# An encoder layer with three mixers: stated engine orders in attention, earlier transfers, column scales as rows

## The chip, the cores and the metric

The kernel runs on one core of one Trainium2 chip. The metric is the device time in microseconds; the kernel before took 1168.31 us (median of three runs, 1164.31 to 1168.86). Engines are named PE (matrix products), ACT (activations and copies), DVE (element-wise and reductions), POOL (element-wise, slower) and SP, the SyncE queue from which nearly all transfers are issued.

## The reference

```python
h = rmsnorm(x, norm_g); u = h @ w_in          # 1024 tokens, 1024 -> 5312 columns
y_conv = conv_module(u_conv, ...)             # GLU, depthwise conv of 31, layer norm, silu
y_ret  = retention_branch(u_ret, ...)         # 4 heads of 128, chunks of 128, two directions
# latent attention: 8 heads, q and k of 128 plain + 64 rotary columns, v of 128
q  = rmsnorm(q_lat, qa_g) @ w_uq;  kv = rmsnorm(kv_lat, kva_g) @ w_ukv
s  = (q_nope . k_nope + rope(q_rope) . rope(k_rope)) * 192 ** -0.5
y_mla = softmax(s) @ v
y = concat([y_conv, y_ret, y_mla]) * silu(u_gate)
out = rmsnorm(x + y @ w_out, final_g)
```

All is float32. The kernel splits each operand of a product into a high part (rounded for PE's faster float32 form) and the rest, and makes three products of them (`mm3`): high by high, high by low, low by high.

## The kernel before

**Stage 1, input projection.** The input stays transposed on chip, eight tiles of 128 columns by 1024 tokens, split into `xH` and `xL` (`load_x`). The weights come in 21 units of 256 columns (`load_unit`, `run_unit`); a unit is 96 matmuls of 128 x 512. While the eight tiles arrive, unit 0 is multiplied tile by tile. `sq_x` squares each tile on ACT and adds the squares, on POOL but for the last tile. `row_rsqrt` turns the sum over the 128 partitions into 1 / root mean square per token: 8 matmuls (16 on the engine) whose weights are every eighth column of the sum and whose moving side is a single column of ones, a scale on DVE, a power on POOL, and a transfer to memory, from which the values are read back as a row over all partitions (`rbc`) and, for the first of the four uses, as columns (`rcol`). Convolution and retention run on DVE and ACT beside later units, handed out in pieces (`tick`).

**Stage 2, attention.** `lat` loads one half of a latent tile, scales it by the row of `row_rsqrt` (on POOL for the first half, `LATP`) and splits it. `g_k`, `g_q`, `g_v` and `g_r` project k, q, v and the rotary part of q for one head or pair of heads; `g_r` sends the rotary part through a transfer that swaps halves, `g_r2` multiplies with the cosine and sine tables on POOL and splits. `g_kr` does the shared rotary key. The weights come through `wload`: transfer, cast on ACT, split on DVE, in one call. A `Unit` is one head by 512 queries, 16 in all, each with eight slots. `qk(i)` makes five matmuls of scores; after every second slot DVE takes the row maximum and ACT the exponential with its row sum. `tr` transposes four 128 x 128 blocks on PE, copies them on ACT and splits them on DVE. `pvs` multiplies with v, `norm` brings the reciprocal of the row sums to a row, `fin` multiplies and stores. Projections of the next heads are spread over the slots by `slot_plan`; they share one bank (`up`) of the accumulation memory, the transposes have two (`pp`).

The row sums go to memory one float at a time and come back as a row:

```python
sp.dma_start(d.rearrange("(t p) -> p t", p=P), self.rs)
rb = mk(fin, [P, HS], tag="rb", bufs=1)
sp.dma_start(rb, d.rearrange("(o s) -> o s", o=1).to_broadcast([P, HS]))
tt(pool, self.g, self.g, rb, MUL)
```

**Stage 3, output projection.** `wo_load` and `y_load` fetch and split a slice of the output weights and of the mixed branches; `wo_mm` multiplies. The first five slices (`NWA`) are loaded in the slots of unit 15, through one raw buffer each for weights and branches. `finish` adds the input, normalises and stores.

**What sets the order.** The body is written in program order, and a planner with its own model of times orders the instructions of every engine (`schedule_with_timeline_sim`); program order is its priority. Each engine then runs its own list strictly in that order. Nothing in the kernel before fixes an order by hand.

Of the kernel before, what the change touches and what calls it, by code (L numbers as in the profile page):

```python
# [37 lines left out]
P_BUFS, PT_BUFS = 3, 2  # L38
# [3 lines left out]
PRO = ["up", "pp", "pp", "pv", "S", "S"]  # L42
LATP = [(i, 0) for i in range(5)]
# [5 lines left out]
SQD = (7,)  # L49
W2_BUFS = 11  # L50
NWARM = 12

# [4 lines left out]
def body(tc, xT, x, w_in, w_uqn, w_uqr, w_uk, w_uv, w_out, vecs, decay, final_g,  # L57
# [72 lines left out]
    def load_x(k, n):  # L130
        tf = mk(cv, [P, S + 2 * HALO], tag="hp", bufs=4)[:, :S]
# [134 lines left out]
    for k in range(KT):  # L266
# [15 lines left out]
        if k > 0:  # L282
            sq_x(k - 1)
    sq_x(KT - 1)
# [11 lines left out]
    def row_rsqrt(ss, scale, eps, o, d):  # L296
        col = mk(const, [P, KT], tag="rrc", bufs=2)
# [9 lines left out]
    row_rsqrt(ssx, 1.0 / D, EPS, rbc, r_dram)  # L307
    sp.dma_start(rcol, r_dram.rearrange("(t p) -> p t", p=P))
# [166 lines left out]
    ident = mk(const, [P, P], tag="ident")  # L475
    sp.dma_start(ident, idm[0])
# [159 lines left out]
    cosm = mk(wt, [P, S], tag="cosm")  # L636
    sinm = mk(wt, [P, S], tag="sinm")

    def wload(src, n, w, tag):
# [3 lines left out]
        sp.dma_start(r, src)  # L643
        act.copy(hi, r)
        split_l(dve, lo, r, hi)
        return hi, lo

    def lw_k(h):
        return wload(w_uk[h], KVT, P, "k")

    def lw_q(h):
        return wload(w_uqn[h], QT, P, "q")

    def lw_r(p):
        return wload(w_uqr[p], QT, P, "r")

    def lw_v(p):
        return wload(w_uv[p], KVT, 256, "v")

    W = {("k", 0): lw_k(0), ("v", 0): lw_v(0)}  # L660
    sp.dma_start(cosm, t_mla[0])
    sp.dma_start(sinm, t_mla[1])
    W["r", 0] = lw_r(0)
    W["q", 0] = lw_q(0)
# [10 lines left out]
    def lat_rows(h):  # L675
        rows[1, h] = row_bc(fin, "rb", lk_dram, h)
        rows[0, h] = row_bc(wt, "xh", lq_dram, h)

    def lat(i, h):
# [5 lines left out]
        tt(pool if (i, h) in LATP else dve, t, t, rows[int(i >= QT), h], MUL)  # L685
# [5 lines left out]
    lat(3, 0)  # L691
    lat(4, 0)
# [6 lines left out]
    for i in range(QT):  # L699
        lat(i, 0)  # L700
# [51 lines left out]
    def g_r(p, hf):  # L752
        o = up3(W["r", p], 0, QT, hf)
        xr = mk(wt, [P, HS], tag="xr")
        xs = mk(wt, [P, HS], tag="xs")
        act.copy(xr, o)
# [3 lines left out]
        rst[p, hf] = xr, xs  # L760

    def g_r2(p, hf):
        xr, xs = rst.pop((p, hf))
        tt(pool, xr, xr, cosm[:, half(hf)], MUL)
        tt(pool, xs, xs, sinm[:, half(hf)], MUL)
# [3 lines left out]
        a, b = sc("QA", 3, F32R), sc("QB", 3, F32R)  # L769
# [24 lines left out]
    class Unit:  # L794
# [6 lines left out]
        def qk(self, i):  # L801
# [13 lines left out]
            if j == 1:  # L815
                nm = mk(at, [P, 1], tag="nm", bufs=4)
                dve.tensor_reduce(nm, self.S, axis=AX.X, op=MAX, negate=True)  # L817
                p = mk(at, [P, S], tag="P", bufs=P_BUFS)
                act.activation(p, self.S, AF.Exp, bias=nm, accum_out=self.rs[:, t:t + 1])  # L819
                self.p.append(p)  # L820
# [12 lines left out]
        def norm(self):  # L833
            i = self.h * 2 + self.qh
# [3 lines left out]
            d = tc.dram_tile([HS], F32, name=f"rs_dram{i}")  # L838
            sp.dma_start(d.rearrange("(t p) -> p t", p=P), self.rs)
            rb = mk(fin, [P, HS], tag="rb", bufs=1)  # L840
            sp.dma_start(rb, d.rearrange("(o s) -> o s", o=1).to_broadcast([P, HS]))
            tt(pool, self.g, self.g, rb, MUL)

        def pvs(self, j):
            if j == 0:
                self.pv = ps("pv")
            p, c = self.h // 2, (self.h % 2) * P
            ph, pl = self.PT[j]
            for i in range(4):
                vh, vl = vv[p, 4 * j + i]  # L850
                mm3(self.pv, vh[:, c:c + P], vl[:, c:c + P], ph[:, i], pl[:, i], j + i == 0, j + i == 4)
# [5 lines left out]

    g_k(0, 0)
    lat_rows(1)
    lat(3, 1)  # L860
    lat(4, 1)
    g_v(0, 0)
    g_k(0, 1)
    g_r(0, 0)
    for i in range(QT):
        lat(i, 1)
    g_q(0, 0)
    g_kr()
    g_r2(0, 0)
    g_r(0, 1)  # L870
    g_r2(0, 1)

    lxx.close()
    sxx = ExitStack()
    def slot_plan(u):
        p, r = u // 4, u % 4
        a, b = 2 * p, 2 * p + 1
        last = p == MH // 2 - 1
        if r == 0:
            return {0: [lambda: W.update({("k", b): lw_k(b)}), lambda: g_q(a, 1)],  # L880
                    4: [lambda: g_v(p, 1)], 5: [lambda: g_v(p, 2)],
                    6: [lambda: W.update({("q", b): lw_q(b)})],
                    7: [lambda: g_v(p, 3)]}
        if r == 1:
            d = {0: [lambda: g_k(b, 0)], 1: [lambda: g_k(b, 1)], 4: [lambda: g_q(b, 0)]}
            if not last:
                d[2] = [lambda: W.update({("r", p + 1): lw_r(p + 1)})]
                d[6] = [lambda: g_r(p + 1, 0)]
                d[7] = [lambda: W.update({("v", p + 1): lw_v(p + 1)})]
            return d  # L890
        if r == 2:
            d = {0: [lambda: g_q(b, 1)]}
            if not last:
# [253 lines left out]
```

## Time and profile before

| | |
|---|---|
| median of three runs | 1168.31 us |
| the profiled execution | 1162.01 us |
| its span, first to last instruction | 1160.2 us |
| PE busy | 1115.4 us (96%) |
| DVE busy | 729.8 us (63%) |
| ACT busy | 408.2 us (35%) |
| POOL busy | 171.3 us (15%) |
| mean granted PE clock | 0.984 |
| moved by transfers | 101.33 MB |

A matmul's end is modelled in the trace, so busy PE overlaps from one matmul to the next; how far apart they start tells the rate. The clock of PE has two levels, 2.4 and 1.2 GHz, and the mean of a stretch tells how much of it ran at which. Releasers are inferred: "<-" names what ended an idle stretch last.

### The profile page before, as it was taken

Reading aid. Unit: us, or ns where it says so; the run is one execution under the profiler, and the core shown is the slowest. Engines: PE = TensorE matmul, PEld = TensorE weight load, DVE = VectorE, ACT = ScalarE, POOL = GpSimd, SP = SyncE. Lnnn points to the kernel's source line nnn. Section 1 sums busy time; section 2 is a strip of 40 time slices with the busy share of each in tenths; the row PEclk is TensorE's granted clock in tenths of the full one; section 3 lists DMA queues with packets and bytes.
Section 4 is the critical chain, followed back from the end, with each engine's and each line's share of the span. In section 5 each row is a group of like instructions: output and inputs, shape, how many; then the busy total and the mean of one; then the engine's idle time right before and its main releaser. Section 6 shows DMA issues by size and latency. Waiting matters only on the chain. (4 is left out here: it accounts for less than half of the span.)

```text
span 1160.2 us, 14263 instructions
## 1 busy us (share of the span) xinstructions
PE 1115.4 (96%) x5548; PEld 933.9 (80%) x5548; DVE 729.8 (63%) x998; ACT 408.2 (35%) x721; POOL 171.3 (15%) x147
## 2 busy tenths in 40 slices
PE   7999999999999999998899999899999979999997
PEld 6888888888898899886678787688778857888886
DVE  6699999997647785746765564555455553345033
ACT  6221222121334134223654453454454443333022
POOL 4300000212220442023201101010110000001000
PEclk9999999998999999999999999999999999999999
DMA  7212223221262122226212212121211242654213
GB/s 261 92 37 73 91 83 117 87 86 46 73 227 91 46 73 69 88 72 227 86 17 74 47 43 53 35 50 35 51 52 29 31 133 56 227 172 150 68 36 109
DMA packets 55491, 101.33 MB, mean 87 GB/s; under 512 B 15584, under 2 KB 19440, under 8 KB 55424
## 3 DMA queue, kind: packets, MB, share of 16 engines
q1 hardware_dynamic: 55376, 100.35, 27.6%
q8 instruction: 43, 0.70, 0.4%
q14 instruction: 24, 0.20, 0.1%
q0 software_dynamic: 48, 0.08, 0.1%
HBM read 74.14 MB, written 24.17 MB: 85 GB/s over the span
## 5 line engine op out<-in xcount | busy, mean ns | idle before, releaser
L176 PE MATMUL ps<-xL,wh 128*128 128x512 f32 (+1 forms) x612 | 240.2, 393 | 3.2 <-DVE xL L63 3.0
L177 PE MATMUL ps<-xH,wl 128*128 128x512 f32 (+1 forms) x612 | 239.6, 392 | 1.9 <-DVE wl L63 1.9
L175 PE MATMUL ps<-xH,wh 128*128 128x512 f32 (+1 forms) x612 | 238.9, 396 | 2.2 <-ACT xH L139 1.6
L63 DVE SCALAR_TENSOR_TENSOR acc<-hp,cwh,acc 128x1024 f32<-128x1024 f32 x120 | 153.3, 1317 | 0.3 <-DVE rrc L301 0.2
L176 PEld LDWEIGHTS ps<-xL,wh 128*128 128x128 f32 x612 | 116.6, 190 | 27.6 <-DVE xL L63 4.2
L177 PEld LDWEIGHTS ps<-xH,wl 128*128 128x128 f32 x612 | 116.1, 190 | 26.5 <-DVE wl L63 2.6
L175 PEld LDWEIGHTS ps<-xH,wh 128*128 128x128 f32 x612 | 116.0, 190 | 26.6 <-ACT xH L139 1.8
L63 DVE SCALAR_TENSOR_TENSOR PL<-ps,PH 128x512 fp32r<-128x512 f32 x128 | 85.7, 685 | 48.7 <-ACT PH L830 48.4
L175 PE MATMUL ps<-woH,yh 128*128 128x512 f32 (+1 forms) x264 | 99.2, 389 | 7.6 <-ACT yh L936 7.4
L176 PE MATMUL ps<-woL,yh 128*128 128x512 f32 (+1 forms) x264 | 101.4, 387 | 0.0
L177 PE MATMUL ps<-woH,yl 128*128 128x512 f32 (+1 forms) x264 | 100.3, 387 | 0.0
L830 ACT CAST PH<-ps 128x512 fp32r<-128x512 f32 x128 | 72.6, 590 | 69.9 <-PE ps L828 69.3
L817 DVE TENSOR_REDUCE nm<-ps 128x1 f32<-128x1024 f32 x64 | 78.1, 1221 | 29.8 <-PE ps L814 29.3
L819 ACT ACTIVATE P<-ps,nm 128x1024 f32<-128x1024 f32 x64 | 71.8, 1122 | 26.3 <-DVE nm L817 24.8
L828 PE MATMUL ps<-ident,P 128*128 128x128 f32 x512 | 73.2, 274 | 4.6 <-DVE PL L63 4.5
L828 PEld LDWEIGHTS ps<-ident,P 128*128 128x128 f32 x512 | 61.5, 141 | 18.0 <-DVE PL L63 6.9
L166 ACT CAST wh<-wraw 128x1024 fp32r<-128x1024 f32 x40 | 42.1, 1051 | 95.0 <-PE ps L176 92.1
L66 POOL TENSOR_TENSOR g<-g,rb 128x512 f32<-128x512 f32 x16 | 20.6, 1289 | 362.2 <-DMA rb<-rs_dram 201.4
L175 PEld LDWEIGHTS ps<-woH,yh 128*128 128x128 f32 x264 | 49.7, 188 | 19.2 <-ACT yh L936 8.4
L63 DVE SCALAR_TENSOR_TENSOR wl<-wraw,wh 128x1024 fp32r<-128x1024 f32 (+2 forms) x45 | 55.4, 1232 | 8.2 <-ACT wh L166 7.4
L177 PEld LDWEIGHTS ps<-woH,yl 128*128 128x128 f32 x264 | 49.7, 188 | 10.8 <-DVE yl L63 0.7
L176 PEld LDWEIGHTS ps<-woL,yh 128*128 128x128 f32 x264 | 49.7, 188 | 10.4
(280 smaller groups left out, 2056.9 us busy)
## 6 DMA issues: line engine op xcount, KB each, us to landing
wraw<-in_w_in_dram SPq DMA_DIRECT2D x40, 512.0 KB, 3.4
wor<-in_w_out_dram SPq DMA_DIRECT2D x16, 512.0 KB, 4.5
g_dram<-ga SPq DMA_DIRECT2D x29, 256.0 KB, 2.0
yr<-y_dram SPq DMA_DIRECT2D x18, 256.0 KB, 4.7
g<-g_dram SPq DMA_DIRECT2D x16, 256.0 KB, 3.4
rb<-rs_dram SPq DMA_DIRECT2D x16, 256.0 KB, 4.9
y_dram<-osb SPq DMA_DIRECT2D x16, 256.0 KB, 2.4
z<-in_x_dram SPq DMA_DIRECT2D x8, 512.0 KB, 3.7
```

The costliest lines, as they stand in the source:

```text
L63: eng.scalar_tensor_tensor(o, a, s, b, op0=op0, op1=op1)
L66: eng.tensor_tensor(o, a, b, op=op)
L166: act.copy(hi, t)
L175: pe.matmul(o, sh, mh, start=first, stop=False, skip_group_check=skip)
L176: pe.matmul(o, sh, ml, start=False, stop=False, skip_group_check=skip)
L177: pe.matmul(o, sl, mh, start=False, stop=last, skip_group_check=skip)
L817: dve.tensor_reduce(nm, self.S, axis=AX.X, op=MAX, negate=True)
L819: act.activation(p, self.S, AF.Exp, bias=nm, accum_out=self.rs[:, t:t + 1])
L828: pe.transpose(o[:, c * P:(c + 1) * P], self.p[t][:, (4 * j + c) * P:(4 * j + c + 1) * P], ident)
L830: act.copy(ph, o)
```

## The change

- From the first attention projection on, PE, ACT, DVE and SP run in program order (`manual_schedule`), up to the end of the attention; PE also to the end of the kernel. POOL, and everything before, is still ordered by the planner.
- The body of attention is put in a new order: projections and slots move, each slot makes its transposes one slot later, the exponential is emitted behind the transposes of its slot (`ex`), `pvs` goes in four parts over slots 2 to 5, `norm` splits into `rec` and `norm`.
- A weight load is split into `w_dma` and `w_cv`, which stand in different slots. The rotary tables are no longer kept whole; each `g_r` fetches the half that it needs.
- Row sums are transposed on PE, copied as four rows, and travel through POOL's queue. `row_rsqrt` reads contiguous weights, transposes its columns on PE and stores rows; the first use keeps its columns as `rcol`.
- Squares of the input come after all eight tiles, all added on DVE; tiles 4 to 7 have buffers of their own. The first halves of the latents are scaled on DVE.
- The first five slices of output weights are loaded and split in unit 14, slots 1 to 7; products with them fill slots of unit 15 and the end of attention.

```diff
-P_BUFS, PT_BUFS = 3, 2
+P_BUFS, PT_BUFS = 2, 3
+MAN = {mybir.EngineType.Activation, mybir.EngineType.DVE, mybir.EngineType.SP}
-        tf = mk(cv, [P, S + 2 * HALO], tag="hp", bufs=4)[:, :S]
+        tf = mk(cv, [P, S + 2 * HALO], tag="hp", bufs=4)[:, :S] if k < 4 else mk(cv, [P, S], tag="acc", bufs=4)
-            tt(dve if k in SQD else pool, ssx, ssx, tf, ADD)
+            tt(dve, ssx, ssx, tf, ADD)
-        if k > 0:
-            sq_x(k - 1)
-    sq_x(KT - 1)
+    for k in range(KT):
+        sq_x(k)
...
-            pe.matmul(c[:, n:n + 1], ss.rearrange("p (q n) -> p n q", n=KT)[:, n, :], ones[:, 0:1], start=True, stop=True)
+            pe.matmul(c[:, n:n + 1], ss[:, n * P:(n + 1) * P], ones[:, 0:1], start=True, stop=True)
         dve.tensor_scalar(col, c[:, :KT], scale, eps, op0=MUL, op1=ADD)
         pool.tensor_tensor(col, col, eps_c[:, :KT], op=ALU.pow)
-        sp.dma_start(d.rearrange("(p n) -> p n", n=KT), col)
+        pe.transpose(c[:KT, P:2 * P], col, ident)
+        row = mk(cv, [P, HS], tag="cb", bufs=2)[:KT, :P]
+        act.copy(row, c[:KT, P:2 * P])
+        sp.dma_start(d.rearrange("(n p) -> n p", p=P), row)
...
+    def w_dma(tag, i):
+        src, n, w = WSRC[tag]
         r = mk(wt, [P, HS], tag="wr", bufs=2)[:, :n * w].rearrange("p (n w) -> p n w", n=n)
+        sp.dma_start(r, src[i])
+        WR[tag, i] = r
+
+    def w_cv(tag, i):
+        src, n, w = WSRC[tag]
+        r = WR.pop((tag, i))
...
         act.copy(hi, r)
         split_l(dve, lo, r, hi)
+        W[tag, i] = hi, lo
...
-        tt(pool if (i, h) in LATP else dve, t, t, rows[int(i >= QT), h], MUL)
+        tt(dve, t, t, rows[int(i >= QT), h], MUL)
...
+        def rec(self):
             self.g = mk(fin, [P, HS], tag="g", bufs=2)
             sp.dma_start(self.g, g_dram[8 + self.h][:, half(self.qh)])
             dve.reciprocal(self.rs, self.rs)
+        def norm(self):
+            d = tc.dram_tile([HS], F32, name=f"rs_dram{self.h * 2 + self.qh}")
+            c = ps("pp")
+            pe.transpose(c[:4, :P], self.rs, ident)
+            row = mk(at, [4, P], tag="rr", bufs=1)
+            act.copy(row, c[:4, :P])
+            pool.dma_start(d.rearrange("(t p) -> t p", p=P), row)
             rb = mk(fin, [P, HS], tag="rb", bufs=1)
+            pool.dma_start(rb, d.rearrange("(o s) -> o s", o=1).to_broadcast([P, HS]))
             tt(pool, self.g, self.g, rb, MUL)
...
+    tail = ExitStack()
+    tail.enter_context(tc.manual_schedule(engines={mybir.EngineType.PE}))
+    inner = ExitStack()
+    if MAN:
+        inner.enter_context(tc.manual_schedule(engines=MAN))
+    g_kr()
+    w_dma("k", 1)
+    lat_rows(1)
     g_k(0, 0)
+    g_v(0, 0)
     lat(3, 1)
+    g_v(0, 1)
     lat(4, 1)
+    g_r(0, 0)
+    g_q(0, 0)
     g_k(0, 1)
+    w_cv("k", 1)
+    w_dma("q", 1)
+    g_r2(0, 0)
     for i in range(QT):
         lat(i, 1)
...
+        if r == 2:
+            return {0: [lambda: g_q(b, 1)], 2: C_("v", p + 1), 3: D_("q", a + 2), 4: C_("k", a + 2), 5: D_("k", b + 2),
+                    6: C_("q", a + 2) + [lambda: g_r2(p + 1, 0), lambda: g_k(a + 2, 0)], 7: [lambda: g_k(a + 2, 1)]}
+        return {0: [lambda: g_r(p + 1, 1)], 1: [lambda: g_q(a + 2, 0)], 2: C_("k", b + 2), 3: D_("q", b + 2),
+                6: [lambda: g_r2(p + 1, 1), lambda: g_v(p + 1, 0)]}
...
-            plan = {1 + k: [lambda k=k: wo_load(k), lambda k=k: y_load(0, k)] for k in range(NWA)}
+            plan = {1: [lambda: dma_k(0)]}
+            for k in range(NWA):
+                plan[3 + k] = [lambda k=k: cv_k(k)] + ([lambda k=k: dma_k(k + 1)] if k < NWA - 1 else [])
+        if u == NUN - 1:
+            ob = [None, None, None, [None, ps("up")]]
+            plan = {i: [lambda k=k: wo_mm(3, k, 1)] for k, i in enumerate((0, 1, 6, 7, 7))}
+            plan[7].append(lambda: wo_mm(3, 3, 1))
         for i in range(8):
             cur.qk(i)
+            if prev and i == 0:
+                prev.rec()
+            if prev and i == 1:
+                prev.norm()
+            q = (i - 3) % 8
+            if i >= 3:
+                cur.tr(q // 2, q % 2)
+            elif prev:
+                prev.tr(q // 2, q % 2)
+            if i % 2:
+                cur.ex(i // 2)
+            if prev and 2 <= i < 6:
+                prev.pvs(i - 2)
+            if prev and i == 5:
+                prev.fin()
             for f in plan.get(i, []):
                 f()
...
+    prev.rec()
+    prev.tr(2, 1)
+    prev.norm()
+    ob[0] = bank_pair(0)
+    for k in range(NWA):
+        for c in range(2):
+            wo_mm(0, k, c)
     prev.tr(3, 0)
     prev.tr(3, 1)
```

## Rows read from the trace of the kernel before

**Rows 1.** Busy time by stage; columns: stretch, its length, each engine's busy time (instructions), clock, transfers.

```profile
0.00:43.00 43.00, 35.24 (x160) 28.67 (x161) 33.64 (x48) 24.04 (x31) 17.57 (x21) 0.96 0.59 202
43.00:52.00 9.00, 9.00 (x34) 7.93 (x33) 1.39 (x2) 0.73 (x1) 1.68 (x1) 0.81 0.32 114
...
259.00:309.00 50.00, 50.00 (x205) 42.36 (x204) 33.85 (x45) 7.75 (x11) 12.90 (x8) 0.90 0.19 64
...
522.00:571.00 49.00, 40.85 (x169) 31.31 (x168) 32.85 (x44) 20.86 (x39) 14.49 (x10) 0.93 0.55 179
571.00:915.00 344.00, 330.55 (x1718) 275.28 (x1716) 191.99 (x277) 169.26 (x319) 43.97 (x34) 0.99 0.18 43
915.00:990.00 75.00, 66.52 (x312) 52.13 (x313) 36.32 (x48) 30.72 (x52) 2.64 (x3) 0.98 0.34 85
990.00:1131.00 141.00, 141.00 (x615) 115.06 (x614) 48.20 (x71) 37.96 (x65) 8.09 (x12) 1.00 0.39 133
```

**Rows 2.** What PE waited for, 0 to 43 us: total, times, longest.

```profile
PE ps L176 <- DVE xL L63: 3.0, 1, 3.0
PE ps L177 <- DVE wl L63: 1.9, 1, 1.9
```

**Rows 3.** Timeline of DVE and POOL in the start: start, length, engine, operation.

```profile
12.37 1.29 DVE L63 SCALAR_TENSOR_TENSOR xL<-hp,vec,xH 128x1024 fp32r<-128x1024 f32 x1 [0.17 <-ACT xH L139]
...
13.38 8.66 POOL L66 TENSOR_TENSOR cm<-cm,hp 128x1024 f32<-128x1024 f32 x3 [11.34 <-ACT hp L148]
...
19.76 3.36 DVE L63 SCALAR_TENSOR_TENSOR xL<-hp,vec,xH 128x1024 fp32r<-128x1024 f32 x1
```

**Rows 4.** Timeline of PE at 259 us.

```profile
259.76 3.74 PE L300 MATMUL ps<-ones,lss 128*128 128x1 f32 x16
...
267.17 0.77 PE L175 MATMUL ps<-xH,wh 128*128 128x512 f32 x1
267.74 0.63 PE L176 MATMUL ps<-xL,wh 128*128 128x512 f32 x1
268.17 0.63 PE L177 MATMUL ps<-xH,wl 128*128 128x512 f32 x1
```

**Rows 5.** Timeline of PE in attention, eight transposes and what follows.

```profile
923.74 1.04 PE L828 MATMUL ps<-ident,P 128*128 128x128 f32 x8
924.53 0.48 PE L810 MATMUL ps<-kH,qH 128*128 128x512 f32 x1
```

**Rows 6.** The line of the power: count, shortest, median and longest in ns.

```profile
L302 POOL TENSOR_TENSOR rrc<-rrc,epsc x4: 1637/1661/2636, 47.6 to 305.5; 128x8 f32<-128x8 f32 x4
```

**Rows 7.** Timeline, rotary part of the first query.

```profile
558.05 0.59 ACT L756 COPY xr<-ps 128x512 f32<-128x512 f32 x1
...
568.15 0.47 PE L813 MATMUL ps<-K,QA 128*128 128x512 f32 x1 [1.77 <-DVE QA L63]
```

**Rows 8.** Timeline, a late weight load and the row sums.

```profile
751.88 0.51 ACT L644 CAST whr<-wr 128x384 fp32r<-128x384 f32 x1 [8.84 <-DMA wr<-in_w_uqr_dram]
...
916.01 0.37 SPq L839 DMA_DIRECT2D rs_dram<-rs  x1
...
930.63 1.28 POOL L66 TENSOR_TENSOR g<-g,rb 128x512 f32<-128x512 f32 x1 [23.22 <-issue]
```

**Rows 9.** Page, costliest groups: busy us, mean ns of one, idle before.

```profile
L63 DVE SCALAR_TENSOR_TENSOR PL<-ps,PH 128x512 fp32r<-128x512 f32 x128 | 85.7, 685 | 48.7 <-ACT PH L830 48.4
...
L830 ACT CAST PH<-ps 128x512 fp32r<-128x512 f32 x128 | 72.6, 590 | 69.9 <-PE ps L828 69.3
L817 DVE TENSOR_REDUCE nm<-ps 128x1 f32<-128x1024 f32 x64 | 78.1, 1221 | 29.8 <-PE ps L814 29.3
L819 ACT ACTIVATE P<-ps,nm 128x1024 f32<-128x1024 f32 x64 | 71.8, 1122 | 26.3 <-DVE nm L817 24.8
```

**Rows 10.** Timeline of SP, output weights.

```profile
933.87 0.33 SPq L923 DMA_DIRECT2D wor<-in_w_out_dram  x1
...
939.91 0.33 SPq L923 DMA_DIRECT2D wor<-in_w_out_dram  x1
```

More of the change, by code (lines that the diff above doesn't have):

```diff
@@ L41 @@
 LTB = 3
-PRO = ["up", "pp", "pp", "pv", "S", "S"]
-LATP = [(i, 0) for i in range(5)]
+PRO = ["up", "pp", "pp", "pv", "S", "S", "up", "pp"]
 MAIN2 = ["pp", "pp"]
@@ L676, in lat_rows @@
         rows[1, h] = row_bc(fin, "rb", lk_dram, h)
-        rows[0, h] = row_bc(wt, "xh", lq_dram, h)
+        if h:
+            t = sc("QB", 3)
+            sp.dma_start(t, lq_dram[half(1)].rearrange("(o s) -> o s", o=1).to_broadcast([P, HS]))
+            rows[0, 1] = t
+        else:
+            rows[0, 0] = row_bc(wt, "xh", lq_dram, 0)
     def lat(i, h):
@@ L690, in body @@
     lat_rows(0)
-    lat(3, 0)
-    lat(4, 0)
+    for i in range(QT + KVT):
+        lat(i, 0)
     for h in range(2):
@@ L755, in g_r @@
         xs = mk(wt, [P, HS], tag="xs")
+        cs = [mk(wt, [P, HS], tag=g) for g in ("cosm", "sinm")]
+        for i in range(2):
+            sp.dma_start(cs[i], t_mla[i][:, half(hf)])
         act.copy(xr, o)
@@ L877, in slot_plan @@
         a, b = 2 * p, 2 * p + 1
-        last = p == MH // 2 - 1
+        more = p < MH // 2 - 1
+        D_ = lambda t, i: [lambda: w_dma(t, i)]
+        C_ = lambda t, i: [lambda: w_cv(t, i)]
         if r == 0:
[L880 to L883, printed above, removed]
-        if r == 1:
[L885 to L889, printed above, removed]
-            return d
+            if p == 0:
+                d = {0: [lambda: g_q(a, 1)], 1: [lambda: g_r(0, 1)], 2: [lambda: g_v(0, 2)], 3: [lambda: g_v(0, 3)],
+                     4: [lambda: g_k(b, 0)] + C_("q", b), 6: [lambda: g_r2(0, 1)]}
+            else:
+                d = {0: [lambda: g_q(a, 1)], 1: [lambda: g_k(b, 0)], 4: C_("q", b), 6: [lambda: g_v(p, 1)],
+                     7: [lambda: g_v(p, 2)]}
+            if more:
+                d[5] = D_("r", p + 1)
+            return d
@@ L891, in slot_plan @@
+        if r == 1:
+            d = {1: [lambda: g_q(b, 0)], 6: [lambda: g_k(b, 1)]}
+            if p:
+                d[0] = [lambda: g_v(p, 3)]
+            if more:
+                d.update({2: C_("r", p + 1), 3: D_("v", p + 1), 5: D_("k", a + 2), 7: [lambda: g_r(p + 1, 0)]})
+            return d
+        if not more:
+            return {0: [lambda: g_q(b, 1)]} if r == 2 else {}
         if r == 2:
[L892 to L897 removed]
@@ L909, in body @@
         plan = slot_plan(u)
-        if u == NUN - 1:
-            sxx.close()
+        if u == NUN - 2:
+            for f in plan.pop(0):
+                f()
             wtx.close()
@@ L931, in y_load, with y_cv @@
                     t = mk(rp[0], [P, HS], tag="yr", bufs=rp[2])
+                sp.dma_start(t, y_dram[k][:, half(hf)])
+                return t
+            def y_cv(hf, k, t):
                 pool_ = pa if k % 8 < NYA else rp[0]
@@ L993, in body @@
         y_load(0, k)
-    ob += [bank_pair(i) for i in range(2, 4)]
+    ob[2] = bank_pair(2)
     for k in range(NWA):
-        for st in range(2, 4):
-            for c in range(2):
-                wo_mm(st, k, c)
+        for c in range(2):
+            wo_mm(2, k, c)
+    ob[3][0] = ps("pv")
+    for k in range(NWA):
+        wo_mm(3, k, 0)
     for k in range(NWA, 8):
```

145 lines of the change are left out of this document (54 added, 91 removed).

## The prediction

> **What bounds the kernel now.** I read the busy time by stage first, then who waited for whom, then the timeline at the places where TensorE (PE) stands still. In the undisturbed stretch from 990 to 1131 us PE starts 615 matmuls in 141 us, 0.229 us each, and never stands [rows 1]; PE is the bound, and nearly all its work is the same after the change. So only what PE loses can move the time: its idle time, plus (1 - granted clock) times the length where the clock is down. By stage [rows 1]: 0 to 43 us, 7.8 idle and 1.7 clock; 43 to 52, 1.7 clock; 259 to 309, no idle but 5.0 clock; 522 to 571 (the entry into attention), 8.2 idle and 3.4 clock; 571 to 915 (units 0 to 13), 13.5 idle and 3.4 clock; 915 to 990 (the last two units), 8.5 idle and 1.5 clock. That is some 55 us, and no step can win more than its own part.
>
> The profiled execution took 1162.0 us (span 1160.2, about 2 around it); the median is 1168.3. I work out a difference against the profiled one and take it off the median.
>
> **The start.** PE's two long waits there are for a DVE split, 3.0 and 1.9 us [rows 2]. That split took 1.29 us alone and 3.36 us while POOL added squares, and POOL spent 8.66 us on three adds from 13.38 on [rows 3]. The change takes all adds from POOL and puts all squares behind the eight loads; loads 4 to 7 get tiles of their own, so they wait for no square. DVE gets six adds more (about 1.3 us each by the split's length, 8 us), off PE's path: what needs them is the row scale, and the second unit's matmuls (96 x 0.229 = 22 us) cover it; without that cover, 8 us would be late. Gone: 4.9 us of waits and most of the 1.7 of clock. I take **-5.5**, from -7 to +2 (the loads may be what is late next).
>
> **Column scales as rows.** Four times, 16 matmuls with one moving column run with weights picked eight floats apart. Two of these runs last 7.41 us (259.76 to 267.17) [rows 4], 0.232 us per matmul, so 64 take 14.8. Afterwards the weights are contiguous. No row has contiguous weights with one column; the nearest is the transpose, 128 contiguous weight columns, eight in 0.79 us [rows 5], 0.10 each. With 0.11 the 64 take 7.0: **-7.6**. Bounds: 0, if the step is not what costs, to -11 at half a transpose. Right behind these runs PE's matmuls are 0.43 us apart in place of 0.229 [rows 4], at the lower of PE's two clocks, 1.2 GHz: seven of them, 1.4 us, at each of three places (one in 43 to 52, two in 259 to 309 [rows 1]), 4.2 in all. The runs halve, so I take half of it off, **-2.5** (0 to -4.2). Added: a transpose in each of the four and in each of 16 units, 20 x 0.11 = **+2.2**. The four wait for POOL's power, 1.66 us [rows 6]; PE is held only if no other matmul stands between: **+1.5** (0 to 6.6).
>
> **Entry into attention.** The rotation tables no longer travel there whole, and the first five latent scalings leave POOL for DVE. But PE, ACT, DVE and SyncE now run in program order. The order is: K rope, one k, two v, one rope projection, one q, one k, then the first score tile, which needs the rotated query. From the evacuation of that projection to the matmul that uses it took 10.1 us (558.05 to 568.15) [rows 7]: a transfer, three POOL steps, a split. Queued on PE in between are 9 + 6 + 3 matmuls at 0.23, 4.1 us. On ACT the evacuation itself now stands behind the scaling of a latent tile that waits for DVE (about 2 us). So PE stands about 10.1 + 2 - 4.1 = 8 us. Then three latent tiles are scaled behind the rotated query on DVE (three times 0.7 + 0.7 + 0.7 in turn with ACT, 6.5 us) before the next q can end: 5 us more. With 2 for the first tiles that makes 15 us, against 11.6 idle and clock now, which count some 1.3 too little, since a modelled matmul end covers the first 0.17 of each gap: **+2**, from -5 (planned as well as now, without the 5 us) to +6 (the clock falls too).
>
> **Units 0 to 13.** The largest single loss begins on SyncE: ACT stood 8.84 us for a weight load (until 751.88), which was queued behind a row-sum transfer, and PE ran dry behind ACT. Such row-sum transfers take 14.6 us from issue to their use (916.01 to 930.63) [rows 8]. Afterwards weights are fetched two to five slots ahead and the sums go as four rows through POOL's queue. A slot is 5 score matmuls (1.15 us), 4 transposes (0.44), in four of eight slots 6 value matmuls (1.4), and at most one projection (0.23 x 9 or 6). I followed one unit of each kind through ACT (copy 0.59, exponential 1.12) and DVE (split 0.69, maximum 1.22) [rows 9]. Scores, maximum, exponential (3 us) have more than a slot before their transposes; no stall. The single bank of the projections stalls PE in two places: in the third unit of each head pair, slot 6, ACT and DVE first do a weight, the rope's four copies and splits, so the two k projections and the next one lose 2.0 us (three times); a v projection in neighbouring slots 7 and 0 loses 0.5 (three times). With 1.5 for unit 0 and 2 for late sums that is 11 against 16.9: **-6**, from -13 to +6 (2 us more in half the units).
>
> A rule of the Trainium skill speaks against POOL's queue (SBUF — State Buffer, section "SBUF: two separate sides"): while DVE runs an operation that takes the port pair it shares with POOL, the descriptors of a transfer issued from POOL can't be written. By it the two transfers of a unit would each wait for one DVE step at most, an estimate of 2 x 0.7 us, inside the slack; the trace shows the shared port only from the other side, DVE stretched from 1.29 to 3.36 us by POOL [rows 3].
>
> **The last two units.** Loads and conversion of five slices of the output weights move from unit 15 to unit 14, slots 3 to 7. They have one buffer: the next load is issued when the slice before is split. Load, cast, split turn in 6.04 us (933.87 to 939.91) [rows 10]. The slots last 3, 3, 3, 1.6, 1.6 us. In stated order ACT and DVE stand in slot 4 until the load lands, with the unit's copies and maxima behind them. The chain starts 8.4 us after slot 1, its fifth split ends at 8.4 + 4 x 6.04 + 3 = 35.6, and only then come the reciprocal and the transpose of the sums, for which PE waits; unhindered PE would be there at 20.3. So 15 us of stall, beside 2 of clock, against 10.0 now (with the same 1.3 hidden, 11 to 12). The partial products pulled into unit 15 fill PE later, not here. **+5**, from -6 (the loads are off the order's way) to +9.
>
> **Sum.** -5.5 - 7.6 - 2.5 + 2.2 + 1.5 + 2 - 6 + 5 = -10.9: 1162.0 becomes 1151, and the median **1157 us**. Projection and end are unchanged.
>
> **Rivals.**
> 1. The order runs clean: no wait of a whole slot stays. For it: PE has over half a slot of slack nearly everywhere. Against: the two chains of 10.1 and 6.04 us lie in the order. It gives -6 -10 +2 -8 -14 -9 = -45, 1123 us.
> 2. Slower: the row sums come too late. They start in slot 1, and the product with them is due at the end of slot 5, 12.4 to 14.5 us on, of which POOL needs 1.3. I reckon 7 to 8 us for the two transfers. If they take as long as now, 14.6 [rows 8], DVE stands 2 to 3 us at the unit's product with every split behind it, and PE loses about 2 us in each of 15 units: +30, 1187 us. It decides at 13 us. For it: each transfer waits for the one before, and POOL's other work stands in the same queue; against: 512 four-byte pieces become four rows.
> 3. The step of the weights costs nothing: the runs of 16 stay as long, and so does the clock. -10.9 + 10.1 = -1: 1167 us, no change that shows. For it: no row shows a short run; against: two to one in spacing to the transposes. The Trainium skill (SBUF — State Buffer, section "Door 1: The DMA port swizzle") speaks against it: only reads within one 16-byte line are at full rate, and eight floats apart each is on another line; the spacing of 0.232 against 0.10 us agrees.
>
> **How the numbers follow.** Forecast 0.45, rival 1 0.20, rival 2 0.20, rival 3 0.15. About 0.5% (6 us) is what can be told from no change here. The forecast's own range is 1146 to 1167 and 0.85 of it is faster, the rest the same; rival 1 is faster, rival 2 slower, rival 3 mostly the same. Faster 0.60, same 0.18, slower 0.22. The range that leaves out a tenth at each end reaches half-way into rivals 1 and 2: 1125 to 1180.
>
> **What would show it.** The runs of 16 at 1.8 us and not 3.7; no POOL add before 40 us, splits at 1.29; PE waiting for the rotated query some 8 us before the first unit; ACT waiting for output-weight loads in unit 14 and PE for the transposed sums about 9 us; the product in slot 5 not waiting for POOL. The forecast is wrong if PE's idle time from 522 to 990 us is under 10 or over 50 us.

## The result, and the profile after

The changed kernel took 1178.55 us (median of 5, 1174.51 to 1179.57) against 1168.31 for the kernel before beside it: ratio 1.009 [1.0065, 1.0114], slower by about 1%. Timed once more, beside later runs, it was 1.013 [1.011, 1.015]. The forecast was 1157 us, faster; the time lies just inside the outer range (1125 to 1180), the direction was wrong. The profiled execution took 1175.6 us.

Busy time of the kernel after by stage; columns as in [rows 1], stretches moved to where the same work now lies:

```profile
0.00:43.00 43.00, 41.65 (x200) 35.75 (x201) 29.61 (x56) 24.63 (x31) 3.47 (x16) 1.00 0.64 225
43.00:52.00 9.00, 9.00 (x42) 7.33 (x41) 2.35 (x4) 1.70 (x3) 2.31 (x1) 1.00 0.16 61
245.00:300.00 55.00, 55.00 (x258) 45.20 (x257) 45.79 (x56) 10.57 (x16) 18.49 (x10) 0.97 0.16 53
503.00:562.00 59.00, 46.49 (x188) 34.21 (x188) 34.89 (x53) 23.89 (x46) 8.87 (x9) 0.88 0.41 131
562.00:919.00 357.00, 346.34 (x1795) 282.84 (x1794) 204.05 (x286) 185.81 (x345) 59.44 (x63) 1.00 0.20 57
919.00:990.00 71.00, 57.89 (x259) 46.20 (x258) 27.44 (x36) 24.94 (x42) 5.98 (x7) 0.88 0.22 71
990.00:1014.00 24.00, 24.00 (x107) 19.83 (x106) 12.46 (x15) 10.55 (x14) 0.00 (x0) 1.00 0.88 317
1014.00:1047.00 33.00, 25.73 (x84) 16.92 (x82) 11.97 (x14) 9.08 (x13) 1.25 (x2) 0.79 0.37 123
1047.00:1140.00 93.00, 90.54 (x390) 72.67 (x389) 24.39 (x42) 18.84 (x38) 5.19 (x9) 1.00 0.25 82
```

The start is nearly full (1.35 us idle, clock 1.00). The surprise is 1014 to 1047: in [rows 1] PE never stands there, and now it is idle for 7.3 of 33 us at a mean clock of 0.79.

Busy time hides part of a gap and counts slow matmuls as busy. So from here I use PE's **loss**: from start to start of consecutive matmuls, less the usual distance of that form (0.229 us for 512 columns). The columns below are stretches of each kernel's own span; "work" is the sum of the usual distances, "first to last" the matmuls' whole. c1 and c2 are the two kernels run again, in two batches in which the kernel before had the same median (1159.6 and 1160.0 us). The runs come from several chips, so each row's ratio is to the kernel before timed beside it.

```
us of loss            0-80  240-320 520-600 600-920 920-1000 1000-end  work   first to last  ratio to before
before, first trace   12.7    3.5    13.5    21.9    13.7     1.1     1084.5   1152.5
after, first trace     4.0    2.8    24.4    16.4    19.4    18.8     1078.7   1165.8     1.009
c2 before again       16.1    3.6    13.7    16.3    12.8     0.9     1084.7   1149.8     1.000
c1 after again         3.5    1.2    24.4    16.3    19.0    19.2     1078.7   1163.6     1.013
e1 proj. planned       4.1    1.2    24.3    16.3    19.0     1.1     1078.7   1146.1     0.998
e7 slice by slice      4.2    2.9    24.6    16.3    19.2     5.5     1079.7   1154.1     1.002
e12 before + order    13.0    4.9    14.8    16.9    15.4    15.2     1084.5   1166.2     1.014
e5 slices spread       4.0    1.2    24.4    16.3     6.5    18.1     1078.7   1150.6     1.001
e3 only PE stated      4.2    4.5    21.3    19.8     2.7    19.4     1078.0   1151.7     1.001
e4 entry               6.2    1.2    23.8    16.4    19.5    18.6     1078.7   1165.8     1.012
e4b entry, space       6.4    1.3    21.8    16.4    18.9    18.6     1077.6   1162.8     1.010
e9 entry, full         4.5    1.2    13.5    20.5    13.7    20.3     1078.3   1153.4     1.002
e2 start + rows        5.8    2.8    15.6    17.3     9.7     1.0     1077.2   1130.6     0.982
e10 rows only         11.2    2.9    14.9    17.0    10.2     1.0     1078.2   1137.0     0.988
e11 start only         6.8    3.6    14.6    15.5    12.7     1.1     1084.3   1140.3     0.993
e6 three edits         6.0    4.3    22.4    16.4     6.5     1.2     1077.9   1136.4     0.985
e8 best                4.5    4.5    13.3    17.6     2.8     1.1     1077.7   1123.2     0.975
```

From c2 to c1: 0-80 us -12.6, 240-320 us -2.4, work -6.0, 520-600 us +10.7, 600-920 us nothing, 920-1000 us +6.2, projection +18.3, in all +14.

The stretches are fixed times, and the kernels reach a unit at different ones: unit 14 begins at 916.2 us in c2, at 907.1 in c1 and at 896.9 in e9. So a stretch can hold a neighbour's loss, and the same loss is counted once more between the first score matmuls of each kernel's own units: from 500 us to unit 1, from there to unit 14, and 85 us from unit 14 on.

```
us of loss             entry, unit 0   units 1-13   units 14, 15
before, first trace        13.2           22.0          13.7
c2 before again            13.4           16.4          12.9
c1 after again             21.2           18.7          19.4
e5 slices spread           21.4           18.6           6.9
e3 only PE stated          19.9           19.3           4.3
e9 entry, full             10.3           18.3          18.4
e2 start + rows            13.0           17.8          11.6
e8 best                    10.3           18.3           4.3
```

By this count the entry with unit 0 costs 7.8 us more from c2 to c1, units 1 to 13 cost 2.3 and the last two units 6.5.

**Projection.** PE's waits in the kernel after, 1014 to 1047 us (total, times, longest), then ScalarE's casts of the last slices of the output weights:

```profile
PE ps L174 <- ACT woH L952: 3.6, 5, 1.1
PE ps L175 <- DVE woL L62: 2.9, 5, 0.8
```

```profile
1018.03 1.05 ACT L952 CAST woH<-wor 128x1024 fp32r<-128x1024 f32 x1 [1.06 <-DMA wor<-in_w_out_dram]
1021.17 1.04 ACT L952 CAST woH<-wor 128x1024 fp32r<-128x1024 f32 x1 [2.10 <-DMA wor<-in_w_out_dram]
1024.17 1.04 ACT L952 CAST woH<-wor 128x1024 fp32r<-128x1024 f32 x1 [1.96 <-DMA wor<-in_w_out_dram]
...
1030.05 1.04 ACT L952 CAST woH<-wor 128x1024 fp32r<-128x1024 f32 x1 [2.08 <-DMA wor<-in_w_out_dram]
```

A slice is ready every 3 us. `finish(0)`, in program order, wants slices 8 to 15 for one half of one row block: three matmuls, 0.69 us, per slice. PE takes each slice as it comes and waits for the next, while all other banks' matmuls, whose slices are there, stand behind it. From 1024.3 us on, in the fifth such wait, the clock is at 1.2 GHz for 13.65 us. In the kernel before, the last cast began later, at 1035.67, and PE lost nothing: the planner had put other banks' matmuls between.

**Entry.** PE's waits from 515 to 570 us, then the chain that the first score tile waits for (QA holds the split of the rotated query, lH the high part of a latent):

```profile
PE ps L814 <- DVE QA L62: 7.7, 1, 7.7
PE ps L174 <- ACT lH L686: 2.7, 2, 1.8
PE ps L174 <- DVE xr L62: 1.6, 1, 1.6
```

```profile
539.60 0.57 ACT L757 COPY xr<-ps 128x512 f32<-128x512 f32 x1
...
548.15 0.62 ACT L769 CAST xh<-xr 128x512 fp32r<-128x512 f32 x1 [5.96 <-POOL xr L65]
...
549.63 0.77 PE L814 MATMUL ps<-K,QA 128*128 128x512 f32 x1 [7.67 <-DVE QA L62]
```

**Last two units.** The loads of the slices, and what PE waits for at their end:

```profile
928.03 0.33 SPq L948 DMA_DIRECT2D wor<-in_w_out_dram  x1
...
933.97 0.33 SPq L948 DMA_DIRECT2D wor<-in_w_out_dram  x1
...
940.15 0.33 SPq L948 DMA_DIRECT2D wor<-in_w_out_dram  x1
```

```profile
946.82 0.37 PE L845 MATMUL ps<-ident,rs 128*4 128x128 f32 x1 [7.36 <-DVE rs L840]
```

The cycle of [rows 10] stands again, 5.9 and 6.2 us, now with the reciprocal and PE's transpose in order behind its fifth turn.

### The profile page after: what moved, and what is told of

It reads as the page before. It is cut to its first block, busy times and chain, and to the rows that moved or that the text cites. A ratio compares the mean times of both kernels' runs of the same rounds, so it can differ in the third digit from the quotient of the medians.

```text
span 1173.7 us, 14356 instructions
## 1 busy us (share of the span) xinstructions
PE 1119.2 (95%) x5568; PEld 925.4 (79%) x5568; DVE 731.1 (62%) x1009; ACT 420.5 (36%) x741; POOL 168.0 (14%) x168
## 4 chain that ended last, share of the span: by engine, by line
PE 81%; DVE 6%; DMA 5%; ACT 5%; issue 1%; SPq 0%; POOL 0%; POOLq 0%; ACTq 0%; DVEq 0%
PE ps L174 22%; PE ps L175 21%; PE ps L176 21%; PE ps L832 4%; DMA wor<-in_w_out_dram 4%; PE ps L815 2%; PE ps L813 2%; PE ps L811 2%; PE ps L812 2%; PE ps L814 2%; DVE nm L818 1%; DVE woL L62 1%; ACT P L823 1%; ACT woH L952 1%; DVE vL L62 1%
## 5 line engine op out<-in xcount | busy, mean ns | idle before, releaser
L834 ACT CAST PH<-ps 128x512 fp32r<-128x512 f32 x128 | 75.0, 587 | 123.5 <-PE ps L832 123.4
L174 PE MATMUL ps<-woH,yh 128*128 128x512 f32 (+1 forms) x264 | 105.4, 399 | 6.7 <-ACT woH L952 3.6
L175 PE MATMUL ps<-woL,yh 128*128 128x512 f32 (+1 forms) x264 | 104.1, 394 | 2.9 <-DVE woL L62 2.9
L176 PE MATMUL ps<-woH,yl 128*128 128x512 f32 (+1 forms) x264 | 103.5, 392 | 0.1
L832 PE MATMUL ps<-ident,P 128*128 128x128 f32 x512 | 78.4, 277 | 5.6 <-ACT P L823 3.2
L174 PE MATMUL ps<-PH,vH 128*128 128x512 f32 x128 | 56.0, 437 | 0.0
```

The costliest lines, as they stand in the source:

```text
L174: pe.matmul(o, sh, mh, start=first, stop=False, skip_group_check=skip)
L175: pe.matmul(o, sh, ml, start=False, stop=False, skip_group_check=skip)
L176: pe.matmul(o, sl, mh, start=False, stop=last, skip_group_check=skip)
L832: pe.transpose(o[:, c * P:(c + 1) * P], self.p[t][:, (4 * j + c) * P:(4 * j + c + 1) * P], ident)
L834: act.copy(ph, o)
```

## Experiments

The question is where 25 us lie between the forecast of -10.9 and +14. Theory: three places where a stated order waits for a chain (projection, entry, last two units). Rivals differ by run.

**The projection.** e1 ends the stated order of PE with the attention:

```diff
     inner.close()
+    tail.close()
     atx.close()
...
-    tail.close()
     pax.close()
```

> The changed kernel with one edit: TensorE's stated order ends with the attention, so the output projection is planned again, as before the change. Theory A (the stated order makes TensorE wait for slices 11 to 15 one after the other while matmuls of other banks could run): the 18.8 us that TensorE loses in 1000-1160 us fall to about 1 to 5, 1178.5 - 14 to 18 = 1161 to 1165 us, and the low clock at 1024-1038 us is gone. Rival B (the slices arrive and are converted too late for any order, since the start of their loading moved): the loss stays, 1175 to 1180 us.

1158.33 us, 0.998 [0.996, 0.999]: by the changed kernel's two ratios (1.009 and 1.013) 13 to 18 us under it; 19.2 us of loss became 1.1. That planning does it and not the mere absence of an order is not yet shown. e7 keeps the order stated, and changes it:

```diff
-            for k in range(8, NG):
+            for k in range(13 if st < 4 else 8, NG):
...
+    for k in range(8, 13):
+        for st in range(4):
+            for c in range(2):
+                wo_mm(st, k, c)
     for st in range(4):
         finish(st)
```

> The changed kernel with TensorE's order still stated to the end, but in the first half of the projection slices 8 to 12 are multiplied into all eight banks, slice by slice, and only 13 to 15 bank by bank. Theory A (it is this order, in which one bank takes slices 8 to 15 one after the other while they arrive every 3 us, that costs the projection its time, not that it is stated): the loss in 1000-1160 us falls from 18.8 to 1-4 us and the low clock there goes, 13 to 17 us under the changed kernel, as where TensorE is planned. Rival B (a stated order as such loses there, because the planner adapts to arrivals in finer steps): 5 to 15 us of the loss stay.

1162.05 us, 1.002 [1.000, 1.003]. PE's row of 1000 to 1100 us in e7:

```profile
1000.00:1100.00 100.00, 98.33 (x427) 79.61 (x427) 34.71 (x51) 27.20 (x46) 4.49 (x8) 1.00 0.44 153
```

The waits for slices and the low clock go; 5.5 us of loss stay, which is the low end of rival B's range. Four waits of 0.94 to 1.04 us, each where a row block waits for VectorE to empty its bank, make up nearly all that e7 loses more than e1 (5.5 against 1.1). So it is this order that costs, and some 4 us are what the planner wins beyond it. e12 adds the order alone to the kernel before:

```diff
     prev.fin()
     atx.close()
+    tail = ExitStack()
+    tail.enter_context(tc.manual_schedule(engines={mybir.EngineType.PE}))
...
         finish(st)
+    tail.close()
```

> The kernel before with one thing added: TensorE runs the output projection in the order in which the program states it. Theory A (this order by itself costs what the changed kernel loses there): 13 to 18 us slower, ratio 1.011 to 1.016, the waits a slice apart near 1018 to 1035 us and a low clock stretch among them. Rival B (it costs only together with the changed kernel's later loads of the slices): 0 to 5 us.

1176.64 us, 1.0137 [1.0106, 1.0167]. PE's waits in e12, same stretch:

```profile
PE ps L175 <- ACT woH L924: 3.0, 3, 1.6
PE ps L176 <- DVE woL L63: 2.0, 4, 0.8
```

The cost needs nothing else of the change.

**The last two units.** e5 converts a slice every second slot of units 14 and 15:

```diff
-            for k in range(NWA):
-                plan[3 + k] = [lambda k=k: cv_k(k)] + ([lambda k=k: dma_k(k + 1)] if k < NWA - 1 else [])
+            cvp = {3 + 2 * k: [lambda k=k: cv_k(k)] + ([lambda k=k: dma_k(k + 1)] if k < NWA - 1 else [])
+                   for k in range(NWA)}
```

> The changed kernel with the five early slices of the output weights converted every second slot of units 14 and 15 instead of every slot of unit 14 (one raw buffer, whose reload takes about 6 us, a slot 5.6 us). Theory A (ScalarE and VectorE in a stated order wait for each slice's transfer, and the exponentials, copies and reciprocals behind them make TensorE wait 3.35, 2.18 and 7.53 us): the 19.4 us of loss in 920-1000 us fall to 8 to 12, and the clock with it, 1178.5 - 7 to 11 = 1167 to 1171 us. Rival B (the waits come from the row sums' and exponentials' own chains): 1176 to 1179 us; where slice 4 then comes too late for the projection, slower.

1163.54 us, 1.001 [1.000, 1.003]. PE's row of 920 to 1000 us in c1, then in e5:

```profile
920.00:1000.00 80.00, 67.51 (x299) 54.13 (x298) 32.30 (x42) 26.73 (x43) 4.84 (x6) 0.89 0.34 115
```

```profile
920.00:1000.00 80.00, 76.09 (x354) 61.99 (x353) 39.59 (x51) 33.08 (x53) 4.86 (x6) 0.98 0.46 162
```

Loss 6.5 against 19.0, less than the 8 to 12 expected, and slice 4 came in time. e3 asks which engine's order it was:

```diff
-MAN = {mybir.EngineType.Activation, mybir.EngineType.DVE, mybir.EngineType.SP}
+MAN = set()
```

> The changed kernel in which ScalarE, VectorE and SyncE are planned as before the change, and only TensorE keeps its stated order, to the end. Theory A (the projection's 18.8 us of loss come from TensorE's order alone; the waits of units 14 and 15 from ScalarE and VectorE standing in order behind the slices' transfers): 1000-1160 us lose 14 to 19 as in the changed kernel, 920-1000 us 8 to 12 instead of 19.4; 520-600 us stay at 20 to 26, because the first rotary query waits for a copy on ScalarE that no order of the others brings forward; the whole 5 to 12 us under the changed kernel. Rival B (the stated order of ScalarE and VectorE is what keeps the 14 middle units short, 16.4 us of loss against 21.9): those units lose 22 or more again and the whole is no better than the changed kernel.

1160.57 us, 1.001 [0.999, 1.002]. 920-1000 us lose 2.7, less than expected: what the changed kernel loses there is the order of the others, and the projection's loss (19.4) is PE's. The 19.8 against 16.3 from 600 to 920 us look like a gain of the others' stated order, but most of it lies at the stretch's ends: unit 1 loses 3 us before 600 us in c1, and unit 14 of e3 loses 1.7 before 920. Units 1 to 13 by themselves lose 19.3 in e3, 18.7 in c1 and 16.4 in c2. A gain of that order there is not shown.

**The entry.** e4 moves the first rotary product up, multiplies the three latents before it scales and splits them, and puts values 2 and 3 of unit 0 ahead of the second query:

```diff
     lat_rows(1)
+    g_r(0, 0)
     g_k(0, 0)
...
-    g_r(0, 0)
...
-    for i in range(QT):
-        lat(i, 1)
+    lt_ = [lat_a(i, 1) for i in range(QT)]
+    for i in range(QT):
+        lat_b(i, 1, lt_[i])
...
-                d = {0: [lambda: g_q(a, 1)], 1: [lambda: g_r(0, 1)], 2: [lambda: g_v(0, 2)], 3: [lambda: g_v(0, 3)],
+                d = {0: [lambda: g_v(0, 2)], 1: [lambda: g_v(0, 3)], 2: [lambda: g_q(a, 1)], 3: [lambda: g_r(0, 1)],
```

> The changed kernel with the entry into attention in another order: the first rotary product stands right behind the rotary key, so that its chain of copies, transfers and GpSimd products runs beside the first keys and values; the three scaled latents of the second half are multiplied first and split afterwards; in unit 0 the values go ahead of the second query. Theory A (what costs 24.4 us in 520-600 us is the chain of the first rotary query, 7.8 us of wait, then the latents one by one, 4.6 us, and the clock that falls in these waits): the loss falls to 8 to 14 us, 1178.5 - 10 to 16 = 1162 to 1168 us. Rival B (the wait only moves on to the latents or the values behind it): 1173 to 1179 us.

1175.33 us, 1.012 [1.010, 1.014]: nothing gained, the rival held. Timeline of e4:

```profile
536.00 0.59 ACT L763 COPY xr<-ps 128x512 f32<-128x512 f32 x1 [3.94 <-DMA g_dram<-xr]
```

```profile
536.61 2.48 SPq L766 DMA_DIRECT2D xs<-xr  x4
539.14 0.58 SPq L686 DMA_DIRECT2D osb<-l_dram  x1
```

The product was there at 530, but its copy waited for a store of unit 20 that still read the same memory; the rotary transfers waited for the copy, and the latents' loads stood behind them on SyncE. PE then waited 7.5 us for a latent instead. e4b takes both away (`lat_d` is a latent's load alone):

```diff
+        if (p, hf) == (0, 0):
+            t = mk(at, [P, S], tag="P", bufs=P_BUFS)
+            xr, xs = t[:, half(0)], t[:, half(1)]
...
+    lt_ = {i: lat_d(i, 1) for i in (3, 4, 0, 1, 2)}
     g_r(0, 0)
```

> The changed kernel with the entry's order changed as in the run before (first rotary product behind the rotary key, values ahead of the second query in unit 0), and two waits of that run taken away by other space and order: the copy of the product goes to a free buffer of the probabilities instead of one that a store of unit 20 still reads until 536 us, and the loads of all five latents of the second half are issued ahead of the rotary transfers. Theory A (the entry's cost is a chain: copy of the rotary product, its four transfers, three GpSimd products, split; it starts late because its buffer is held and it blocks SyncE's queue): the copy starts near 531-533 instead of 536-540 us, the wait for the first QA falls from 7.8 to 0-3 us, the loss in 520-600 us from 24.4 to 8-15, the whole 9 to 16 us under the changed kernel. Rival B (VectorE's work, some 19 us between 527 and 546, bounds the entry whatever the order): the loss stays at 18 to 24.

1172.31 us, 1.010 [1.009, 1.012]. Timeline of e4b:

```profile
532.17 0.59 ACT L767 COPY P<-ps 128x512 f32<-128x512 f32 x1
...
547.28 0.69 DVE L62 SCALAR_TENSOR_TENSOR QB<-P,xh 64x512 fp32r<-64x512 f32 x1
```

The copy starts 7.4 us sooner, the wait for QA falls only from 7.8 to 4.2, and the values wait 3.9 us for VectorE. The loss of 21.8 lies in rival B's range; expected was too much, for from the copy's start to the end of both splits the chain lasts 15.8 us. e9 gives PE work beside it (values, second query, second rotary product ahead of the scores) and the latents' products to GpSimd:

```diff
-        tt(dve, t, t, rows[int(i >= QT), h], MUL)
+        tt(pool if h else dve, t, t, rows[int(i >= QT), h], MUL)
...
     g_k(0, 1)
+    g_v(0, 2)
...
+    g_v(0, 3)
...
+    g_q(0, 1)
...
     g_r2(0, 0)
+    g_r(0, 1)
```

> The changed kernel with the entry of e4b taken further: GpSimd, idle there until 542 us, multiplies the five latents of the second half; values 2 and 3, the second query and the second rotary product all stand ahead of the first scores, so that TensorE has some 8.5 us more to do while the first rotary query's chain runs. Theory A (that chain, 14.4 us from the copy's end to QA and QB in e4b, is the entry's floor, and only work of TensorE beside it hides it): the wait for QA falls from 4.2 us (7.8 in the changed kernel) to 0-2, the values' 3.9 us to 0-1, the loss in 520-600 us from 21.8 (24.4) to 8-14, with the low clock there 3 to 7 us long instead of 13.65: 10 to 17 us under the changed kernel. Rival B (VectorE's splits, some 17 us from 527 on, stand in the way): loss 16 to 22, at most 8 us under the changed kernel.

1162.82 us, 1.002 [1.000, 1.004], and PE's row of 520 to 600 us in c1, then in e9:

```profile
520.00:600.00 80.00, 64.78 (x296) 48.36 (x295) 46.28 (x67) 36.90 (x68) 12.91 (x11) 0.91 0.26 84
```

```profile
520.00:600.00 80.00, 73.83 (x350) 57.75 (x349) 49.73 (x71) 43.56 (x81) 22.86 (x19) 0.96 0.31 97
```

The first scores wait 0.5 us for QA in place of 7.7; the loss is 13.5, as in the kernel before (13.7). Counted up to unit 1 it is 10.3, against 21.2 in c1 and 13.4 in c2. The 20.5 and 13.7 of the next two stretches are no change of those units: e9's unit 14 begins 10 us sooner, and part of its loss falls before 920 us.

**Start and row scales.** e10 has the row scales alone, e11 the start alone, e2 both, each on the kernel before (the diff's parts ahead of attention).

```diff
-            pe.matmul(c[:, n:n + 1], ss.rearrange("p (q n) -> p n q", n=KT)[:, n, :], ones[:, 0:1], start=True, stop=True)
+            pe.matmul(c[:, n:n + 1], ss[:, n * P:(n + 1) * P], ones[:, 0:1], start=True, stop=True)
...
-            tt(dve if k in SQD else pool, ssx, ssx, tf, ADD)
+            tt(dve, ssx, ssx, tf, ADD)
```

> The kernel before with the column scales as rows alone (contiguous weights for the matmuls of one column, a transpose, one transfer of rows); squares, attention and projection as before. The prediction's terms: -7.6 us for the 64 matmuls, up to -2.5 for the clock behind them, +2.2 for transposes, 0 to 6.6 for the power on GpSimd: -9 to 0 us, most likely -6.4, ratio 0.992 to 1.000. By the run that changed rows and start together (0.982, -21 us) what this run leaves is the start's share: forecast -5.5. Rival: the rows carry more than the matmul time, because the squares' sums reach them in time only then: -12 to -16 us, ratio 0.986 to 0.990.

> The kernel before with the start alone changed: squares added on VectorE, buffers of their own for the later slices of x. The prediction's term: -5.5 us (-7 to +2). By difference of the runs with rows and start (-21) and rows alone (-14): -7. Theory A (it lies in the first 52 us alone): loss in 0-80 us 12.7 to 5-7, the whole 5 to 8 us under the kernel before, ratio 0.993 to 0.9955. Rival (it also changes what is planned in attention): 10 or more, under 0.991.

> The kernel before with only the part of the change that lies ahead of attention: squares added on VectorE with buffers of their own, column scales computed as rows; attention and projection as before. Theory A (the parts add up, each pays where it lies): 8.8 us of loss at the start and 5.8 us of matmul time go, 1168.3 - 14 = 1153 to 1156 us. Rival B (the gain is given back behind it, since the transfers and TensorE's clock fall otherwise): 1163 to 1168 us.

e10 1145.71 us, 0.988 [0.986, 0.989]; e11 1151.34, 0.993 [0.990, 0.996]; e2 1140.39, 0.982 [0.979, 0.985]. They add up: 14 + 8 against 21 us, which is more than e2 was expected to give (12 to 15). e10's 14 us are the rival's number and more than its terms. By the traces (c2 to e10, -12.8): work -6.5, 240-320 us -0.7, and 40-80 us, where the low clock is gone, -2.5. The rest is spread (0-40 us -2.4, 920-1000 us -2.6, 520-600 us +1.2, 600-920 us +0.7), so the rival's cause isn't shown, and the stretch 0-40 us differs as much between the two traces of the same kernel before (11.2 and 13.4). c2 was run for that question:

> The kernel before once more, with a trace from the chip of the runs beside it: ratio 1.000. If part of what the row scales seemed to gain in attention was only that the first trace of before came from another chip, this trace loses 40 to 43 us in 520-1000 us, as e10; if the row scales' own effect reaches there, 47 to 50 as in the first trace.

Ratio 0.9998 [0.998, 1.002]; 42.8 us lost from 520 to 1000 us against 49.1 in the first trace. So what the row scales seemed to gain in attention (42.1 in e10) was the first trace's own.

> The changed kernel once more, as the common measure for the runs beside it: 0.7 to 1.1% over the kernel before, as in its first timing (1.009).

1174.72 us, 1.013 [1.011, 1.015], a little more than expected.

**A version that beats both.** e6 joins e1, e4b and e5; e8 joins e1 and e9 and ends the stated order of ScalarE, VectorE and SyncE at unit 14:

```diff
         if u == NUN - 2:
+            inner.close()
```

> The changed kernel with three edits together: TensorE planned in the projection, the slices spread over units 14 and 15, and the entry of e4b. Theory A (the three places are independent): losses of about 1 in the projection, 6.5 in 920-1000 us and 8 to 15 in 520-600 us, in all 33 to 42 us under the changed kernel, ratio to the kernel before 0.972 to 0.980: with or a little under the run that changes only the start (0.982). Rival B (spreading the slices leaves the projection less to do while slices 5 to 15 arrive, or the gains of one place reappear as waits in the next): 20 to 28 us under the changed kernel, 0.985 to 0.992.

> All that the runs so far point to: the start and the row scales of the change, the entry of e9, the stated order of all four engines kept for units 0 to 13 alone; from unit 14 on ScalarE, VectorE and SyncE are planned, in the projection TensorE too. Theory A (each place by itself): losses of 10 at the start, 8 to 14 in 520-600 us, 16 in units 0 to 13, 3 in 920-1000 us, 1 in the projection: 48 to 56 us under the changed kernel, ratio 0.963 to 0.971, under the run that changes only the start (0.982). Rival B (as e9's): 0.973 to 0.982.

e6 1143.89 us, 0.985 [0.983, 0.987]: faster than the kernel before, not than e2 (0.982); the entry still lost 22.4 where 8 to 15 were expected. e8 1130.74 us, 0.975 [0.973, 0.977]: faster than the kernel before and than e2. Its row of 920 to 1000 us:

```profile
920.00:1000.00 80.00, 78.19 (x363) 63.79 (x363) 35.85 (x45) 32.12 (x48) 4.83 (x6) 1.00 0.47 167
```

The places of e8 lost about what was expected of them (13.3, 17.6, 2.8, 1.1), the start less (4.5 against 10). The total in the expectation was not their sum: by the traces e8 lies 40 us under c1, by the medians 44, not 48 to 56, and the ratio lies where rival B had it. Against e2, which keeps attention as before, e8 loses 2.7 us less in the entry and 7.3 less in the last two units, and nothing less in units 1 to 13.

## Why the prediction was wrong

- **"Projection and end are unchanged"** is the step that failed: +18.3 us. I had read from [rows 1] that PE never stands in 990 to 1131 us and took that for a property of the work. It was one of the planner's order, and the change ended that too; the text even said that PE follows program order, and then followed it only to the end of attention. With this term at 18 the sum is +7, slower.
- **Entry: +2 forecast, +7.8 measured**, counted up to unit 1 (21.2 in c1, 13.4 in c2; the +10.7 of the fixed stretch holds 3 us of unit 1). The chain was right: 10.0 us from the copy (539.60) to the matmul (549.63), of which 8 us of wait were forecast (7.7), then 5 for the latents (4.1) and 2 for the first tiles (3.7). Left out was the clock while PE waits: 3.5 us of slow matmuls, which stood only in the upper bound. The rest, some 2 us, are small gaps that I did not assign.
- **Units 0 to 13: -6 forecast, no gain measured.** Units 1 to 13 lose 18.7 us in c1 and 16.4 in c2. What I worked out for the kernel after was right (11; idle and clock together are 10.7 in 562 to 919 us). The 16.9 of before was not: c2, the same kernel, has 12.9 in the same stretch, so by that count the gain is 2.2:

```profile
571.00:915.00 344.00, 334.56 (x1736) 279.14 (x1735) 193.71 (x279) 171.03 (x322) 43.95 (x34) 0.99 0.17 45
```

- **Last two units: +5 forecast, +6.5 measured**: 13.9 of wait and 5.1 of clock against "15 and 2".
- **Start: -5.5 forecast, -9.9 measured** from 0 to 40 us between c2 and c1; by e11 alone -8 in time. VectorE's splits lost GpSimd's interference and the loads were not late.
- **Row scales: -7.6, -2.5, +2.2, +1.5 forecast.** The runs of 16, kernel after:

```profile
249.10 1.84 PE L299 MATMUL ps<-ones,lss 128*128 128x1 f32 x16
250.81 1.93 PE L299 MATMUL ps<-ones,lsk 128*128 128x1 f32 x16
```

 1.8 us in place of 3.7 [rows 4]: rival 3 falls, and the work, transposes included, is 6.0 us less, against 5.4 forecast. The clock gave 5.1 from c2 to c1 (2.7 in 40-80 us, 2.4 in 240-320), twice the term, but part of that is luck of the trace: with the same row scales, 240-320 us lose 1.2 in c1 and 2.8 to 4.5 in the first trace, e2, e3, e6, e7, e8 and e10, against 3.6 in c2. In e3 the clock behind the runs is still at 1.2 GHz for 6.8 us. What stands against both traces of before are 1.5 to 2.7 us in 40-80 us, where the low clock is gone: about the term, and not twice it. The wait for the power is not seen. By the Trainium skill (SBUF — State Buffer, section "Door 1: The DMA port swizzle") reads within one 16-byte line go at full rate; the trace agrees for weights: contiguous columns cost 0.11 us a matmul, columns eight floats apart 0.23.
- **Rival 2** did not come. Row sums of one unit, kernel after:

```profile
634.79 0.55 POOL L848 DMA_DIRECT2D rs_dram<-rr  x1 [15.88 <-ACT rr L847]
637.16 0.58 POOL L850 DMA_DIRECT2D rb<-rs_dram  x1 [1.81 <-DMA rs_dram<-rr]
...
640.99 1.29 POOL L65 TENSOR_TENSOR g<-g,rb 128x512 f32<-128x512 f32 x1 [0.70 <-DMA rb<-rs_dram]
```

 6.2 us from issue to use where [rows 8] had 14.6 and the forecast 7 to 8 for the transfers. Rival 1 fell at both chains, 7.7 and 6.0 us.

In numbers, from c2 to c1: -10.9 plus 18.3 (projection), 5.8 (entry), 8.3 (units) and 1.5 (last two), less 4.4 (start), 0.6 (work), 2.6 (clock) and 1.5 (power) is +14. That the time still fell inside the outer range is luck: the range reached into rivals 1 and 2, and the mechanism of neither came.

Still open: what part of a stretch's low clock is cause and what effect of the waits. In the entry, the last two units and the projection it is lower where PE waits most, and no run took the one away without the other.

## What to carry to other kernels

Where a written order takes the place of a planned one, walk it to its last instruction, and at each stretch whose inputs arrive one by one, ask which ready work stands behind the first that isn't: a stretch without idle time in the old trace says nothing of the new order there. State an order by hand only where a run shows that it wins, and give the rest back. In units 1 to 13 no run shows it (18.7 us of loss in c1, 19.3 in e3, 16.4 in c2). In the last two units PE's stated order with the other engines planned loses 4.3 us (e3 and e8) against 12.9 in c2; which part of that is the order and which the earlier loads, no run separates. Count a stage between its own instructions and not between fixed times when kernels reach it at different ones. And a small gain read off one trace needs a second trace of the same kernel: one stage differed by 5.6 us.

## What was not expected of the hardware

Sparse waits went with a low clock as well as idle time: eleven waits of 0.65 to 1.31 us between 1018 and 1034 us (the loss at each) stand beside 13.65 us at 1.2 GHz, and in e7, where these waits are gone, the clock of 1000 to 1100 us is 1.00. A transfer of four rows from GpSimd's queue (rs_dram<-rr) landed after 1.6 us at the median in e8, where 512 pieces of four bytes from SyncE's took 9.1 in the kernel before; pieces and queue changed together, and no run parts them.
